# RWKV chunk operands of one layout for heads of both parities, and r and v projected inside the chunk loop, in a two-layer backbone on one core

## The chip, the cores and the metric

One Trainium2 chip, one of its cores. The time is device time in microseconds of one execution of the whole program; the number for a kernel is the median of several executions.

## What is computed

The program is a backbone of two layers over 512 latent and 256 context tokens. Layer 0 mixes by attention, layer 1 by two recurrences; each layer ends in a mixture of 64 experts. The change is in layer 1, in the bidirectional RWKV-7 mixing, whose reference is

```python
r, k, v, z_w, z_a, z_g = ... shift_mix(h @ w_in) ...      # p + mu * (mean of both neighbours - p)
decay = exp(-exp(-softplus(-w_pre) - 0.5)); iclr = sigmoid(...); kk = k * kvec[0] / norm
def rwkv7_step(state, inp):                    # per direction and head, over 768 tokens
    r, w, k, v, kk, a = inp
    sa = einsum('...vk,...k->...v', state, -kk)
    state = state * w + sa (x) (kk * a) + v (x) k
    return state, einsum('...vk,...k->...v', state, r)
```

with 8 heads of 64 channels, two directions, and an output gate and group norm behind it. A second recurrence (mLSTM, 4 heads of 128) runs beside it on other columns of the same projection.

## The kernel before, in words

The kernel computes the recurrence in chunks of 64 tokens. The head index is h = 2j + s: j is one of four 128-column blocks, s the half of the partitions (the parity). Layer 1 goes through four stages.

**Inputs** (`rec_mixed`, from L1673). `project` (L1584) multiplies one 128-column block of the weights with the normalised tokens: each product runs as three fp32r products (L414 to L416, high and low parts), over a context segment of 256 tokens and a latent segment of 512, in k-steps; the result lies in a two-bank PSUM tile `pp`, of which there are two. The weights' high part is cast on ACT (L1593), the low part made on POOL (L1594). `shifted` (L1678) copies the result to a padded tile, adds the neighbours on POOL (L1695), and `mix` (L1699) scales on ACT (L1703) and combines on DVE (L1704). This is done for z (4 blocks), k (4; its norm goes through the reciprocal L1754, and kk to DRAM at L1756), r (4, latent tokens only; L1758 to L1761) and v (4; transposed at L1771, stored to DRAM at L1776). The mLSTM gates (`mlstm_gates`) are a generator of 12 steps, taken one at a time in the loops over k, r and v.

**Chunk loop** (`rec_chunks`, from L2004, called in L1617 to L1621). Six pairs of chunks b and two directions d. `prep` makes the operands: tanh (L2077), plus one on POOL (L2078), a cumulative sum (L2081), two exponentials, the copy of the chunk's last decay to PL (L2088), then ST (L2100 from kk on DVE, L2102 from r on POOL) and BK (L2112, L2113). ST and BK are written by one instruction for each partition half s, since the two parities have their 64-column parts in opposite order (FA, FR in L2011). `pairs` multiplies BK with ST for each chunk q, j and s (L2149; the matmul has L394, the line of the helper `crit`), copies Aab out on ACT (L2154), and masks the rest into ST and Arb on DVE (L2156, L2160), again for each half; it stores Aab, ST, Arb and BT to DRAM with one DMA per tile (`put`, L2048, its issue has L2054). `invert` inverts 16-wide blocks (L2194, L2196) and `merge` joins them (products T, Q, W, TT). The products of each go through PSUM banks `pb` (four of them).

`weave` (L294) draws the steps of several generators in proportion to their stated lengths; that is the order of the program. In the same weaves run the 80 steps of `mlstm_project` (L1781), the projections of the mLSTM's q, k, v and o, in portions written out by hand: `take(9)`, `take(6)`, then 7 and 6. The compiler's scheduler fixes each engine's order in advance from a simulated timeline, with the program's order as priority; at run time every engine keeps that order.

**Rest of the chunks** (L1628, L1629) beside the first mLSTM cells. **Scan** (`rwkv_scan`, from L2245): 12 steps in each direction, that load the chunks' operands, multiply (px), copy X out of PSUM in two halves (L2293), multiply, copy the new V (L2306), update the state (L2319, L2322) and copy or add the output y in two halves (L2334, L2336). `self.copy` takes ACT and DVE in turn (L387, L389). Five steps run beside the mLSTM cells, the others beside a part of the output projection.

After it come the output projection, the router and the second layer's experts, which the change does not touch.

Of the kernel before, what the change touches and what calls it, by code (L numbers as in the profile page):

```python
# [26 lines left out]
NCTX = 256  # L27
# [79 lines left out]
def constants_rec():  # L107
# [6 lines left out]
    low = (p < 64)[:, None]  # L114
    both = [np.where(low, np.concatenate([incl[d], strict[d]], 1), np.concatenate([strict[d], incl[d]], 1))
            for d in range(2)]
# [239 lines left out]
class Kern:  # L356
# [1178 lines left out]
    def rec_project(self, es, x, R):  # L1535
# [72 lines left out]
        with tc.tile_pool(name="rt", bufs=1, reuse_waits="tile") as tp:  # L1608
            self.rec_mixed(tp, project, mu2, nkv, low, r, k_, R)
# [63 lines left out]
    def rec_mixed(self, tp, project, mu2, nkv, low, r, k_, R):  # L1673
# [45 lines left out]
        for j in range(4):  # L1719
            cur = shifted(12 + j, (CT, LT))  # L1720
# [20 lines left out]
        for j in range(4):  # L1741
            next(gates)
# [15 lines left out]
        for j in range(4):  # L1758
            next(gates)
            cur = shifted(j, (LT,))  # L1760
            mix(cur, 0, j, LT, r[:, j])  # L1761
        for j in range(4):
            next(gates, None)
            cur = shifted(8 + j, (CT, LT))
            vT, vt = z(), z()
            for sl in (CT, LT):
                mix(cur, 2, j, sl, vT[:, sl])
            for t0 in (0, 3):
                p = self.bank((128, 3, 128))
                for t in range(3):  # L1770
                    nc.tensor.transpose(p[:, t], vT[:, (t0 + t) * 128:(t0 + t + 1) * 128], self.k_ident)  # L1771
                self.copy(vt[:, t0 * 128:t0 * 128 + 384], p.rearrange("p a b -> p (a b)"))
            next(gates, None)
            for q in range(2):
                for s in range(2):
                    nc.sync.dma_start(R["V"][q::2, s, :, j * 64:(j + 1) * 64].rearrange("c p v -> p c v"),  # L1776
                                      vt[64 * q:64 * q + 64].rearrange("p (c s v) -> p c s v", c=6, s=2)[:, :, s])
# [3 lines left out]
    def mlstm_project(self, tp, project, R):  # L1781
# [5 lines left out]
        def stage(name, n=NTOK, bufs=2):  # L1787
            return tp.tile([128, n], F32, name=name, tag=name, bufs=bufs)
# [13 lines left out]

        for h in range(4):
# [200 lines left out]
    def rec_chunks(self, gp, low, up, kv2, wa2, r, k_, R):  # L2004
# [6 lines left out]
        FA, FR = (half[0], half[1]), (half[1], half[0])  # L2011
# [32 lines left out]
        def par(v, s):  # L2044

            return v.rearrange("p c (j e) t -> p c j e t", e=2)[:, :, :, s]

# [10 lines left out]
        def prep(b, d):  # L2058
# [19 lines left out]
            nc.gpsimd.tensor_scalar(sw, sw, 1.0, None, op0=add)  # L2078
# [12 lines left out]
            ST = tmp("ST", 3, (128, 2, 8, 128))  # L2091
            ST = ST.rearrange("p q h t -> p (q h t)")[:, 0:16 * w].rearrange("p (q h t) -> p q h t", q=2, h=8)
            BK = tmp("BK", 2, (128, 4, 2, 128))
            SA = FA if lat else (half[0], half[0])
            jc = lambda v, s: two(v[half[s]])
            cj = lambda v, s: jc(v, s).rearrange("p j c t -> p c j t")
            dj = lambda v, s: v[half[s]].rearrange("p j c t -> p c j t")
# [13 lines left out]
            for s in range(2):  # L2111
                nc.vector.tensor_tensor(BK[half[s], :, :, FR[s]], jc(ke, s), jc(E2, s), op=mult)  # L2112
                nc.vector.scalar_tensor_tensor(BK[half[s], :, :, FA[s]], jc(aa, s), -0.5, jc(E2, s), op0=mult, op1=mult)  # L2113
            P[b, d] = dict(ST=ST, BK=BK, SA=SA, kk=kk, ke=ke)
# [21 lines left out]
        def pairs(b, d):  # L2136
            lat = b >= 2
            ST, BK, SA = (P[b, d][n] for n in ("ST", "BK", "SA"))
            Aab = tmp("Aab", 4, (128, 2, 4, 64))
            Arb = tmp("Arb", 2, (128, 2, 4, 64)) if lat else None  # L2140
            BT = tmp("BT", 2, (128, 2, 4, 128))

            cs = [slice(0, 128) if lat else FA[s] for s in range(2)]
            ss = [slice(0, 128) if lat else SA[s] for s in range(2)]
            for q in range(2):
                p = self.pair((128, 2, 4, 128))
                for j in range(4):
                    for s in range(2):
# [3 lines left out]
                for s in range(2):  # L2152
                    bh, kh = half[s], half[1 - s]
                    nc.scalar.copy(Aab[bh, q], p[bh, s, :, FA[s]])  # L2154
                    mask = self.k_both[kh, d, cs[s]]
                    nc.vector.tensor_tensor(par(ST[kh], s)[:, q, :, ss[s]], p[kh, s, :, cs[s]],  # L2156
                                            mask[:, None].to_broadcast([64, 4, mask.shape[-1]]), op=mult)
                    if lat:
                        mask = self.k_incl[bh, d]
                        nc.vector.tensor_tensor(Arb[bh, q], p[bh, s, :, FR[s]],  # L2160
                                                mask[:, None].to_broadcast([64, 4, 64]), op=mult)
# [10 lines left out]
            for q in range(2):  # L2172
                p = self.bank((128, 4, 128))
                for j in range(4):
                    self.crit_t(p[:, j], BK[:, j, q], self.k_ident)
                nc.scalar.copy(BT[:, q], p)
                yield
            put(b, d, 1024, BT)
# [66 lines left out]
    def rwkv_scan(self, room, R):  # L2245
# [4 lines left out]
        half = FA = (slice(0, 64), slice(64, 128))  # L2250
# [20 lines left out]
        def step(n, d, Y):  # L2271
# [4 lines left out]
            ST = L[:, 1024 - 8 * w:1024].rearrange("p (h t) -> p h t", h=8)  # L2276
            BT = L[:, 1024:1536].rearrange("p (j t) -> p j t", j=4)
# [5 lines left out]
            if n < 11:  # L2283
                load(n + 1, d)
            px = self.bank((128, 2, 4, 64))
# [178 lines left out]
```

## Time and profile before

| | us |
|---|---|
| median of 3 executions | 2880.4 |
| lowest, highest | 2874.06, 2880.7 |
| the profiled execution | 2889.01 |
| its span, first to last instruction | 2887.2 |

| engine | busy us | share of the span |
|---|---|---|
| PE (matmul) | 2426.5 | 84% |
| PEld (weight load) | 1477.0 | 51% |
| DVE | 1214.1 | 42% |
| ACT | 705.5 | 24% |
| POOL | 661.6 | 23% |

The mean granted clock of TensorE over the span is 0.900 of full speed. Shares over the span mix stages of different limits; layer 1's recurrence lies between about 1400 and 2140 us. An engine's instructions overlap in the timeline, so the busy time of a group is a sum of durations and not a share of the span, while an engine's own busy time in a window counts each moment once.

### The profile page before, as it was taken

What the parts mean: (1) busy time and instruction counts of PE and PEld (TensorE: products, weight loads), DVE (VectorE), ACT (ScalarE), POOL (GpSimd) and SP (SyncE); (2) the same over time, 40 slices, a digit from 0 to 9 for tenths busy, and PEclk for the clock granted to TensorE, in tenths of its full rate; (3) what the DMA queues carried; (4) which work ended last, traced back from release to release, by engine and by line L of the source; (5) the groups of instructions that cost most, each with busy time, mean ns of one, the idle gap of its engine ahead of it and who ended that gap; (6) DMA issues with size and microseconds to landing.
All of it is one profiled execution on the core that took longest, in us unless ns stands there. A gap on an engine that the chain in (4) does not pass through costs nothing. (4 is left out here: it accounts for less than half of the span.)

```text
span 2887.2 us, 45906 instructions
## 1 busy us (share of the span) xinstructions
PE 2426.5 (84%) x18031; PEld 1477.0 (51%) x18031; DVE 1214.1 (42%) x2625; ACT 705.5 (24%) x1556; POOL 661.6 (23%) x618
## 2 busy tenths in 40 slices
PE   7789887979999999994899777766866989988993
PEld 6658664864433443331678666666755323323331
DVE  5742545472122222214753677755576211212214
ACT  3442434231111111112544433412212100000001
POOL 0111010002112122111344454534530111111211
PEclk9899998879999999997899788868966999999996
DMA  8645444659999999995224445588644998999995
GB/s 313 221 126 128 100 132 110 249 224 337 379 342 329 356 338 342 382 347 179 84 75 108 134 128 156 157 223 276 235 163 167 386 396 336 361 395 353 340 406 186
DMA packets 253865, 721.91 MB, mean 250 GB/s; under 512 B 110968, under 2 KB 137336, under 8 KB 194512
## 3 DMA queue, kind: packets, MB, share of 16 engines
q1 hardware_dynamic: 216656, 631.86, 59.7%
q0 software_dynamic: 26336, 67.70, 9.4%
q10 hardware_dynamic: 10656, 19.40, 2.0%
q8 instruction: 143, 2.34, 0.4%
q14 instruction: 74, 0.61, 0.1%
HBM read 636.06 MB, written 107.33 MB: 257 GB/s over the span
## 5 line engine op out<-in xcount | busy, mean ns | idle before, releaser
L1235 PE MATMUL pb<-ew,xT 128*32 128x512 f32 (+2 forms) x3504 | 656.2, 607 | 21.5 <-DMA ew<-in_moe_w_dram 14.7
L1235 PEld LDWEIGHTS pb<-ew,xT 128*32 128x32 f32 (+2 forms) x3504 | 212.0, 127 | 394.5 <-issue 354.9
L1235 PE MATMUL pp<-ew,hT 128*32 128x512 f32 (+2 forms) x1752 | 330.6, 607 | 13.1 <-DMA ew<-in_moe_w_dram 6.0
L1456 DVE SCALAR_TENSOR_TENSOR hs<-s,gate,pb 128x256 f32<-128x256 f32 x86 | 41.3, 480 | 608.0 <-ACT s L1451 596.7
L1225 POOL DMA_INDIRECT xg<-rows,idx x86 | 89.0, 1035 | 857.4 <-PE pp L1279 300.3
L1451 ACT ACTIVATE s<-pb 128x256 f32<-128x256 f32 x96 | 36.3, 383 | 815.0 <-PE pb L1235 785.4
L1270 POOL DMA_INDIRECT acc<-ye,idx x86 | 136.9, 1591 | 327.8 <-issue 109.9
L1235 PEld LDWEIGHTS pp<-ew,hT 128*32 128x32 f32 (+2 forms) x1752 | 101.6, 127 | 194.1 <-issue 174.3
L414 PE MATMUL pp<-h_hi,w_hi 128*128 128x512 f32 (+1 forms) x432 | 161.3, 375 | 4.8 <-DVE mT L389 4.3
L415 PE MATMUL pp<-h_lo,w_hi 128*128 128x512 f32 (+1 forms) x432 | 158.7, 368 | 1.1 <-DVE h_lo L410 1.1
L416 PE MATMUL pp<-h_hi,w_lo 128*128 128x512 f32 (+1 forms) x432 | 158.9, 369 | 0.6 <-POOL w_lo L1594 0.6
L1594 POOL TENSOR_TENSOR w_lo<-w,w_hi 128x512 fp32r<-128x512 f32 x66 | 93.3, 1415 | 170.1 <-ACT w_hi L1593 100.0
L1279 PEld LDWEIGHTS pp<-consts,xg 128*128 128x128 f32 x688 | 79.9, 147 | 77.0 <-issue 55.7
L1279 PE MATMUL pp<-consts,xg 128*128 128x128 f32 x688 | 99.1, 290 | 20.8 <-DMA xg<-rows,idx 7.6
L440 PE MATMUL pb<-ada_w,cz 128*32 128x256 f32 x640 | 56.1, 471 | 52.6 <-DMA ada_w<-in_ada_w_dram 52.6
L414 PEld LDWEIGHTS pp<-h_hi,w_hi 128*128 128x128 f32 x432 | 86.0, 200 | 20.5 <-DVE mT L389 4.4
L1282 DVE COPY xT<-pp 128x512 f32<-128x512 f32 x86 | 59.3, 690 | 88.2 <-ACT xT L1281 88.2
L416 PEld LDWEIGHTS pp<-h_hi,w_lo 128*128 128x128 f32 x432 | 85.5, 198 | 16.3 <-issue 3.4
L415 PEld LDWEIGHTS pp<-h_lo,w_hi 128*128 128x128 f32 x432 | 86.2, 199 | 14.9 <-issue 2.2
L414 PE MATMUL pb<-w_hi,m_hi 128*128 128x256 f32 x256 | 76.8, 303 | 11.6 <-ACT w_hi L409 11.6
L1281 ACT COPY xT<-pp 128x512 f32<-128x512 f32 x86 | 50.3, 585 | 147.7 <-PE pp L1279 146.5
L598 PE MATMUL pb<-consts,P 128*128 128x128 f32 x384 | 70.6, 301 | 9.9 <-ACT P L854 5.3
(515 smaller groups left out, 4610.9 us busy)
## 6 DMA issues: line engine op xcount, KB each, us to landing
ew<-in_moe_w_dram SPq DMA_DIRECT2D x384, 1024.0 KB
ada_w<-in_ada_w_dram SPq DMA_DIRECT2D x48, 1024.0 KB
w<-in_rec_w_dram ACTq DMA_DIRECT2D x66, 256.0 KB
steps<-dL SPq DMA_DIRECT2D x16, 1024.0 KB
acc<-zero SPq DMA_DIRECT2D x12, 1024.0 KB
ew<-acc SPq DMA_DIRECT2D x10, 1024.0 KB
w<-in_att_w_dram SPq DMA_DIRECT2D x18, 512.0 KB
cells<-dM SPq DMA_DIRECT2D x8, 1056.0 KB
```

The lines of the kernel that those rows point to most:

```text
L414: mm(out, l_hi, r_hi, start=start, stop=False)
L415: mm(out, l_hi, r_lo, start=False, stop=False)
L416: mm(out, l_lo, r_hi, start=False, stop=stop)
L440: nc.tensor.matmul(p[32 * g:32 * g + 32], self.cz[:, 4 * a + g, 30 - 2 * i:62 - 2 * i], w[:, 4 * a + g, :], start=i + a == 0, stop=i + 1 = ...
L598: nc.tensor.transpose(t[:, c - c0, :], p[:, c * 128:(c + 1) * 128], self.k_ident)
L1225: nc.gpsimd.indirect_dma_start(out=xg, out_offset=None, in_=self.rows[layer], in_offset=bass.IndirectOffsetOnAxis(ap=idx, axis=0), bounds_ ...
L1235: nc.tensor.matmul(out[s], x[:, s], ws[m], start=start, stop=stop, tile_position=(0, s.start))
L1270: nc.gpsimd.indirect_dma_start(out=self.acc[layer], out_offset=bass.IndirectOffsetOnAxis(ap=idx, axis=0), in_=y, in_offset=None, bounds_ch ...
L1279: columns_of.last = nc.tensor.transpose(p[:, k], xg[:, k * 128:(k + 1) * 128], self.k_ident[:n, :n])
L1281: nc.scalar.copy(out[:, 0:4], p[:, 0:4])
L1282: columns_of.done = nc.vector.tensor_copy(out[:, 4:8], p[:, 4:8])
L1594: nc.gpsimd.tensor_tensor(lo, w, hi.bitcast(F32), op=OP.subtract)
```

## The change

The two parts of ST are now in the order of their source (tensor index o: 0 from kk and r, 1 the masked product), and the same for both parities; so each of the instructions that wrote one half of the partitions is now one for both. Products in `pairs` are split in two: 64 columns of BK at a time, with the output in the half `s ^ o`. The stores of ST and BT to DRAM are split in three each. The decay's last column is made by an exponential on ACT and not copied by DVE; plus one moves from POOL to ACT. In the scan X and y leave PSUM with one instruction each. r and v leave `rec_mixed` and become the first 48 steps of the generator woven into the chunk loop, now of 128 steps; the portions become 13, 9, then 11 and 9, and 60 in the last weave. Gate steps are taken two at a time in the loops over z and k.

```diff
-            blocks = self.mlstm_project(tp, project, R)
+            blocks = self.rec_others(tp, project, mu2, r, R)
...
-                weave(W("prep", at(m), 0), W("pairs", at(m - 1), 1), W("merge", at(m - 2)), take(7 if m else 9))
+                weave(W("prep", at(m), 0), W("pairs", at(m - 1), 1), W("merge", at(m - 2)), take(11 if m else 13))
...
-                      W("bonus", at(m - 1) if m > 2 else None), take(6))
-            weave(W("pairs", at(5), 1), W("merge", at(4)), take(40))
+                      W("bonus", at(m - 1) if m > 2 else None), take(9))
+            weave(W("pairs", at(5), 1), W("merge", at(4)), take(60))
...
         for j in range(4):
+            next(gates)
+            next(gates)
             cur = shifted(12 + j, (CT, LT))
...
-        for j in range(4):
-            next(gates)
-            cur = shifted(j, (LT,))
-            mix(cur, 0, j, LT, r[:, j])
...
+        for j in range(4):
+            yield from shifted(j, 0, j, (LT,), lambda sl, t: r[:, j])
+        for j in range(4):
+            got = []
+            yield from shifted(8 + j, 2, j, (CT, LT), lambda sl, t: got.append(t) or t)
+            vt = tp.tile([128, 6, VW], F32, name="mt", tag="mt", bufs=1)
...
-            nc.gpsimd.tensor_scalar(sw, sw, 1.0, None, op0=add)
+            nc.scalar.activation(sw, sw, AF.Identity, bias=1.0, scale=1.0)
...
+            nc.scalar.activation(R["PL"][:, d, 2 * b:2 * b + 2].rearrange("p q j -> p j q"),
+                                 two(sw)[..., 63 * (1 - d)], AF.Exp, scale=LAM)
             nc.scalar.activation(E2, sw, AF.Exp, scale=-LAM)
-            nc.vector.tensor_copy(R["PL"][:, d, 2 * b:2 * b + 2].rearrange("p q j -> p j q"), E3[..., 63 * (1 - d)])
...
-            for s in range(2):
-                dst = par(ST[half[s]], s)
-                nc.vector.tensor_tensor(dst[:, :, :, SA[s]], dj(E1, s), cj(kk, s), op=mult)
-                if lat:
-                    nc.gpsimd.tensor_tensor(dst[:, :, :, FR[s]], dj(E3, s), cj(r[:, :, ls], s), op=mult)
+            nc.vector.tensor_tensor(ST[:, :, 0, :, half[0]], dj(E1), cj(kk), op=mult)
+            if lat:
+                nc.gpsimd.tensor_tensor(ST[:, :, 0, :, half[1]], dj(E3), cj(r[:, :, ls]), op=mult)
...
-                    for s in range(2):
-                        self.crit(p[:, s, j, cs[s]], BK[half[s], j, q], ST[half[s], q, 2 * j + s, ss[s]],
-                                         start=True, stop=True, tile_position=(64 * s, 0))
+                    for o in range(2):
+                        for s in range(2):
+                            self.crit(p[half[s ^ o], o, j, 0:w], BK[half[s], j, q, half[o]], ST[half[s], q, 0, j],
+                                      start=True, stop=True, tile_position=(64 * s, 64 * (s ^ o)))
...
+                nc.scalar.copy(Aab[:, q], p[:, 0, :, half[0]])
+                mask = self.k_both[:, d, 0:w]
+                nc.vector.tensor_tensor(ST[:, q, 1], p[:, 1, :, 0:w], mask[:, None].to_broadcast([128, 4, w]), op=mult)
...
-            put(b, d, 0 if lat else 512, ST)
+            nc.sync.dma_start(Ld[half[0], :, at:at + 8 * w], ST[half[0]].rearrange("p q o j t -> p q (o j t)"))
+            for o in range(2):
+                a = at + 4 * w * (1 - o)
+                nc.sync.dma_start(Ld[half[1], :, a:a + 4 * w], ST[half[1], :, o].rearrange("p q j t -> p q (j t)"))
...
             X, S = Xs[d], Ss[d]
-            for s in range(2):
-                self.copy(X[half[s]], px[half[s], s])
+            self.copy(X, px[:, 0])
```

BK's writers and the adding and copying of y are joined in the same way as ST and X, and BT's store is split like ST's. In `rec_others` the padded tile and its neighbour sum both come from the tag `mT` of two buffers, which the mLSTM's stages use too, and v's transposed tile from `mt` of one buffer.

## Rows read from the trace of the kernel before

**Rows 1.** Windows view: inputs, chunk loop, scan; busy us (instructions) per engine, clock, DMA.
```profile
1400.00:1564.60 164.60, 159.74 (x817) 125.99 (x817) 79.69 (x87) 78.10 (x132) 74.71 (x107) 0.98 0.25 75
1564.60:1885.00 320.40, 245.68 (x2275) 206.81 (x2275) 228.06 (x404) 128.67 (x320) 155.87 (x107) 0.82 0.52 144
...
1968.00:2140.00 172.00, 131.16 (x1980) 111.45 (x1978) 107.28 (x259) 44.02 (x102) 84.39 (x92) 0.84 0.67 224
```

**Rows 2.** Timeline of PE inside two projections: start us, us, what; first and last of runs.
```profile
1498.69 0.39 PE L414 MATMUL pp<-h_hi,w_hi 128*128 128x512 f32 x1
...
1503.73 0.39 PE L415 MATMUL pp<-h_lo,w_hi 128*128 128x512 f32 x1
...
1525.14 0.28 PE L414 MATMUL pp<-h_hi,w_hi 128*128 128x256 f32 x1
...
1526.38 0.28 PE L416 MATMUL pp<-h_hi,w_lo 128*128 128x256 f32 x1
```

**Rows 3.** Groups by form, inputs stage (busy us, mean ns | idle before, releaser).
```profile
L1771 PE MATMUL pb<-consts,z 128*128 128x128 f32 x24 | 3.9, 272 | 0.0
...
L1754 DVE RECIPROCAL z<-z 128x768 f32<-128x768 f32 x4 | 19.8, 4950 | 3.9 <-ACT z L1753 3.9
```

**Rows 4.** Waits in the chunk loop: who for whom, us in total, times, longest.
```profile
ACT Aab L2154 <- DVE Arb L2160: 42.8, 12, 7.5
...
PE pp L394 <- DVE ST L2156: 13.1, 3, 6.7
...
PE pb L1799 <- DVE mT L389: 11.7, 1, 11.7
```

**Rows 5.** Groups of DVE in the chunk loop, by form; the last over 1565 to 1900.
```profile
L2113 DVE SCALAR_TENSOR_TENSOR BK<-aa,sw 64x512 f32<-64x512 f32 x24 | 25.6, 1066 | 0.1
L2100 DVE TENSOR_TENSOR ST<-decay,kk 64x512 f32<-64x512 f32 x24 | 24.5, 1019 | 0.2
L2112 DVE TENSOR_TENSOR BK<-ke,sw 64x512 f32<-64x512 f32 x24 | 23.8, 993 | 2.8 <-POOL ke L2109 2.4
...
L2156 DVE TENSOR_TENSOR ST<-pp,consts_rec 64x512 f32<-64x512 f32 x28 | 19.2, 686 | 12.6 <-ACT Aab L2154 12.2
...
L2160 DVE TENSOR_TENSOR Arb<-pp,consts_rec 64x256 f32<-64x256 f32 x28 | 11.8, 422 | 0.6
L2088 DVE COPY PL<-decay 128x8 f32<-128x8 f32 x12 | 10.8, 898 | 0.9 <-ACT decay L2086 0.8
...
L2229 DVE TENSOR_TENSOR W<-pb,T 128x512 f32<-128x512 f32 x9 | 6.2, 688 | 2.5 <-PE pb L394 2.3
```

**Rows 6.** Groups of POOL in the chunk loop, by form.
```profile
L2102 POOL TENSOR_TENSOR ST<-decay,rk 64x512 f32<-64x512 f32 x16 | 24.5, 1528 | 0.6
...
L2078 POOL TENSOR_SCALAR sw<-sw 128x512 f32<-128x512 f32 x12 | 18.0, 1498 | 35.8 <-ACT sw L2077 32.4 <-PE pp L394 3.2 <-DVE W L2229 0.2
```

**Rows 7.** Timeline of PE: products of the chunks, 64-row operands.
```profile
1674.40 1.16 PE L394 MATMUL pp<-ST,BK 64*128 64x128 f32 x16
...
1678.86 1.15 PE L394 MATMUL pb<-T,Aab 64*64 64x64 f32 x32
...
1718.25 2.08 PE L394 MATMUL pp<-ST,BK 64*128 64x128 f32 x16 [1.78 <-ACT mT L387]
```

**Rows 8.** Scan: a wait in total, and the timeline of one pair of copies.
```profile
ACT steps L387 <- DVE steps L389: 51.6, 35, 6.2
...
2064.44 0.42 DVE L389 COPY steps<-pb 64x256 f32<-64x256 f32 x1
...
2064.94 0.37 ACT L387 COPY steps<-pb 64x256 f32<-64x256 f32 x1 [0.90 <-DVE steps L389]
```

**Rows 9.** SP's queue: an issue, issue time of a kind (min/median/max ns), a wait.
```profile
1514.89 0.36 SPq L1756 DMA_DIRECT2D dK<-z  x1
...
L2054 SPq DMA_DIRECT2D dL<-BT x12: 359/463/1235, 1597.3 to 1920.9; - x12
...
SPq L2164 <- ACT Aab L2154: 42.8, 9, 17.9
```

More of the change, by code (lines that the diff above doesn't have):

```diff
@@ L113, in constants_rec @@
     far = (s // 16) != (t // 16)[None, :]
-    low = (p < 64)[:, None]
-    both = [np.where(low, np.concatenate([incl[d], strict[d]], 1), np.concatenate([strict[d], incl[d]], 1))
-            for d in range(2)]
+    both = [np.concatenate([strict[d], incl[d]], 1) for d in range(2)]
     c["far"] = np.concatenate([strict[0] & far, strict[1] & far], 1)
@@ L1671, in out_ahead, with rec_mixed @@
             yield
-    def rec_mixed(self, tp, project, mu2, nkv, low, r, k_, R):
+    def rec_mixed(self, tp, project, mu2, nkv, low, k_, R):
         nc, i = self.nc, self.i
@@ L1741, in rec_mixed @@
         for j in range(4):
-            next(gates)
+            next(gates, None)
+            next(gates, None)
             cur = shifted(4 + j, (CT, LT))
@@ L1757, in rec_mixed, with rec_others @@
                               kn.rearrange("p (b t) -> p b t", b=6))
-        for j in range(4):
-            next(gates)
-            cur = shifted(j, (LT,))
-            mix(cur, 0, j, LT, r[:, j])
[L1762 to L1774, printed above, removed]
-                for s in range(2):
-                    nc.sync.dma_start(R["V"][q::2, s, :, j * 64:(j + 1) * 64].rearrange("c p v -> p c v"),
-                                      vt[64 * q:64 * q + 64].rearrange("p (c s v) -> p c s v", c=6, s=2)[:, :, s])
         for _ in gates:
             pass
-    def mlstm_project(self, tp, project, R):
+    def rec_others(self, tp, project, mu2, r, R):
         nc = self.nc
@@ L1785, in mlstm_project, with stage, shifted @@
         M = R["M"]
-        def stage(name, n=NTOK, bufs=2):
-            return tp.tile([128, n], F32, name=name, tag=name, bufs=bufs)
+        def stage(name, n=NTOK):
+            return tp.tile([128, NTOK + 4], F32, name=name, tag=name, bufs=2)[:, :n]
+        def shifted(b, n, j, segs, dst):
+            pad, sh = stage("mT", NTOK + 4), stage("mT")
+            nc.gpsimd.memset(pad[:, 0:1], 0.0)
+            nc.gpsimd.memset(pad[:, NCTX + 1:NCTX + 3], 0.0)
+            nc.gpsimd.memset(pad[:, NTOK + 3:NTOK + 4], 0.0)
+            at = lambda sl, n=1: slice(sl.start + n + 2 * (sl.start > 0), sl.stop + n + 2 * (sl.start > 0))
+            yield from project(b, lambda sl, p: nc.scalar.copy(pad[:, at(sl)], p), segs)
+            for sl in segs:
+                t = sh[:, sl]
+                nc.gpsimd.tensor_tensor(t, pad[:, at(sl, 0)], pad[:, at(sl, 2)], op=OP.add)
+                nc.scalar.activation(t, t, AF.Copy, scale=mu2[:, 0, n, j:j + 1])
+                nc.vector.scalar_tensor_tensor(dst(sl, t), pad[:, at(sl)], mu2[:, 1, n, j:j + 1], t,
+                                               op0=OP.mult, op1=OP.add)
+            yield
         c6 = lambda v: v.rearrange("p (c t) -> p c t", c=v.shape[1] // 128)
@@ L2147, in pairs @@
                 for j in range(4):
-                    for s in range(2):
-                        self.crit(p[:, s, j, cs[s]], BK[half[s], j, q], ST[half[s], q, 2 * j + s, ss[s]],
-                                         start=True, stop=True, tile_position=(64 * s, 0))
+                    for o in range(2):
+                        for s in range(2):
+                            self.crit(p[half[s ^ o], o, j, 0:w], BK[half[s], j, q, half[o]], ST[half[s], q, 0, j],
+                                      start=True, stop=True, tile_position=(64 * s, 64 * (s ^ o)))
                 yield
[L2152 to L2161, printed above, removed]
+                nc.scalar.copy(Aab[:, q], p[:, 0, :, half[0]])
+                mask = self.k_both[:, d, 0:w]
+                nc.vector.tensor_tensor(ST[:, q, 1], p[:, 1, :, 0:w], mask[:, None].to_broadcast([128, 4, w]), op=mult)
+                if lat:
+                    nc.vector.tensor_tensor(Arb[:, q], p[:, 0, :, half[1]],
+                                            self.k_incl[:, d, None].to_broadcast([128, 4, 64]), op=mult)
                 yield
@@ L2175, in pairs @@
                     self.crit_t(p[:, j], BK[:, j, q], self.k_ident)
-                nc.scalar.copy(BT[:, q], p)
+                nc.scalar.copy(BT[:, q].rearrange("p s j v -> p j s v"), p.rearrange("p j (s v) -> p j s v", s=2))
                 yield
-            put(b, d, 1024, BT)
+            nc.sync.dma_start(Ld[:, :, 1024:1280], BT[:, :, 0].rearrange("p q j v -> p q (j v)"))
+            for s in range(2):
+                nc.sync.dma_start(Ld[half[1 - s], :, 1280:1536], BT[half[s], :, 1].rearrange("p q j v -> p q (j v)"))
             P[b, d] = dict(A=Aab, kk=P[b, d]["kk"], ke=P[b, d]["ke"])
@@ L2287, in step @@
                 j, s = h // 2, h % 2
-                self.crit(px[half[s], s, j], ST[:, h, FA[s] if lat else half[0]], V[:, s, j], start=h < 2,
+                self.crit(px[half[s], 0, j], ST[:, s, j, half[0]], V[:, s, j], start=h < 2,
                                  stop=not lat, tile_position=(0, 64 * s), skip_group_check=True)
@@ L2330, in step @@
                 y = Y[:, c - 4]
-                for s in range(2):
-                    o = half[1 - s]
-                    if n <= 7:
-                        self.copy(y[o], px[o, s])
-                    else:
-                        nc.vector.tensor_tensor(y[o], y[o], px[o, s], op=add)
+                if n <= 7:
+                    self.copy(y, px[:, 1])
+                else:
+                    nc.vector.tensor_tensor(y, y, px[:, 1], op=add)
                 yield
```

54 lines of the change are left out of this document (30 added, 24 removed).

## The prediction, made before the changed kernel was run

> **What bounds the kernel now.** I read the windows first, since shares over the whole span mix stages [rows 1]. In the inputs stage, 164.6 us, PE is busy for 159.7 of them at a granted clock of 0.98: nothing but PE work sets its length. In the chunk loop, 320.4 us, no engine is full: PE 245.7, DVE 228.1, POOL 155.9, ACT 128.7, at a clock of 0.82. There 74.7 us of PE's time are idle, and part of the rest runs at the lower of the two clock levels: the same 16 instructions take 1.16 us at one place and 2.08 at another [rows 7]. The scan, 172.0 us, is full on no engine either.
>
> The waits of the loop tell why [rows 4]. ACT's copy of Aab stood 42.8 us behind DVE's Arb, which reads another half of the same PSUM tile, so the readers of a product take turns; PE in turn waited 13.1 us for the mask product on DVE to free the tile, and 11.7 us in one piece for a projection's copy in DVE's queue. The groups of DVE show the load [rows 5]: ST and BK are written by 24 half-height instructions each, 73.9 us in three groups. A full-height product of 512 columns costs 688 ns and a half-height one 686 ns: height is free, so two halves joined cost one.
>
> **The change, part by part.** *r and v leave the inputs stage.* One latent matmul of 512 columns follows the next after (1503.73 - 1498.69) / 22 = 0.229 us, a context one of 256 columns after (1526.38 - 1525.14) / 11 = 0.113 us [rows 2]. A block has 24 of each. r: 4 x 24 x 0.229 = 22.0 us. v: 4 x 24 x (0.229 + 0.113) = 32.8 us. v's transposes: 24 x 272 ns, less the overlap that a duration contains, about 3 us [rows 3]. Together 58 us, and since that stage is all PE, it gets shorter by these 58. Against it stands its new end: the k blocks each carry a reciprocal of 4.95 us on DVE [rows 3], and the last store of kk, issued at 1514.89 [rows 9], stood some 50 us ahead of the loop's start; now the loop's first operands need it at once. r's projections cover that for PE. I charge 3 us, bounds 0 and 10 (two reciprocals). The gates' steps, now two at a time, are DVE work inside a stage of some 109 us that has at most 79.7 us of it: 0; if DVE fell behind there, z's products would wait for it, up to the same 10.
>
> *The same 58 us of PE work enter the loop.* The rest of r and v comes with it: weight loads on ACT's queue, casts, low parts and neighbour sums on POOL, scaling on ACT, combining on DVE, 16 stores on SP. r and v are 8 of the 17 blocks of the inputs stage, so at most half of what that stage has: ACT 39 us, POOL 37, DVE (79.7 - 19.8) / 2 = 30 [rows 1, 3].
>
> *DVE gets lighter.* Joined halves: 73.9 / 2 = 37.0 for ST and BK, 9.6 for the mask, 5.9 for Arb; PL's copy leaves, 10.8 [rows 5]. That is 63 us off 228.1, plus at most 30 from r and v: under 196 us. *POOL* loses 18.0 (plus one) and 12.2 (half of ST) [rows 6] and gains up to 37: under 163. *ACT* gains up to 39, plus one (bounded by POOL's 18.0) and twelve small exponentials, and loses half of the Aab copies: under 190. All three stay below two thirds of 320.
>
> *The products in pairs double in number.* A latent pass (16 of them: 4 chunk pairs, 2 directions, 2 chunks) has 8 products of 128 columns now, 1.16 us; afterwards 16 with half the weights' width. T's row has 16 products of 64 x 64 in 1.15 us [rows 7]: 16 products can be no dearer than twice 1.16 and hardly cheaper than once. Extra: 0 to 16 x 1.16 = 18.6; the 8 context passes take T's form exactly, extra 0 to 9, and I take 0 by that row. In sum 9 us, bounds 0 and 28.
>
> The Trainium skill, TensorEngine Tiling (Array Packing), section Tiling Modes, says that four 64 x 64 tiles load and multiply independently of each other. By that the extra would be 0 and PE's work 9 us less; no row of before has four such tiles in turn.
>
> *SP* issues 48 more DMAs (two each for ST and BT, 12 times) and v's 16: 64 x 0.46 = 30 us. It is in order; in the loop it waited 42.8 us for Aab alone [rows 9], so the issues fit there, but a store in front of the inversion's load delays it by about 1 us a pair. I take 0; without that cover it would be 30.
>
> *What the loop then takes.* PE: 245.7 + 58 + 9 = 313 us at the present clock mix. At a mean of 0.82 between 0.5 and 1, some 36% of the time is at the lower level, and so 88 us of the 245.7, which would take half at the upper: 269 to 313, about 290 if the extra filling lifts the clock halfway. Nothing else is near. The lower bound is 269 / 0.97, the filling of the inputs stage: 277, 43 shorter than now. The upper is everything on top: 320 + 67 = 387. I take 320, no change, which is 290 at 91% filling: better than now, since the readers of a product no longer queue (two banks, each with its own reader first) and the waits for DVE lose their cause, but not the inputs stage's 97%, since pairs and projections share two PSUM tiles. Likely 295 to 345.
>
> *Scan.* X left PSUM by DVE at 2064.44 and then by ACT until 2065.31; such turns cost ACT 51.6 us of waiting [rows 8]. One copy of 0.42 saves 0.45 us in each of 24 steps: 0 to 10.8. As two directions run beside each other, half: 5. y's joined copies lie off the chain; I cost them at 0.
>
> Sum: -58 + 3 + 0 - 5 = **-60 us**. The profiled execution took 2889.0, so 2829 in its terms; it lies 8.6 above the median of 2880.4, which gives 2820. A difference under 0.3% (8.6 us) can't be told from none.
>
> **The rivals.** *The loop hangs on its chain, not on PE.* Then lighter DVE and POOL shorten it although PE has more to do, down to its bound of 277: -58 + 3 - 43 - 5 = -103, that is 2777. For it: the idle 74.7 us, and every wait of [rows 4] is on something that shrinks. Against: it needs PE full almost throughout, in a program order whose waits vary.
>
> *The work is only moved.* If PE's idle time can't be filled, since it lies where filling is not allowed (a projection needs one of two PSUM tiles that pairs hold), the loop takes 387: -58 + 3 + 67 - 5 = +7, that is 2887, within 0.3% of before; halfway it would be 2854. For it: PE waited although projections were there to be run. Against: the product's readers now free the tiles sooner.
>
> *Slower: projections that wait to be evacuated.* r and v leave PSUM through padded tiles that share two buffers with the mLSTM's stages, sum and all; the next block's copy waits until the block before is combined on DVE, and the tile of PSUM stays taken meanwhile. Before, one such wait for a copy cost PE 11.7 us in one piece [rows 4]. If the work is moved without filling, and one in three of the 24 blocks waits so long, 8 x 11.7 = 94: 2887 + 94 = 2981. From the forecast, it decides from 60 / 11.7, five such waits, on. Against: only one in 16 blocks before, and DVE is lighter.
>
> **How the numbers follow.** Forecast (loop 295 to 345, so 2795 to 2845): 0.62. Chain rival, 2795 and below: 0.17. Only moved, 2845 to 2889: 0.15. Slower: 0.06. The likeliest gives **2820**. The range 2783 to 2858 takes in the forecast, nearly all of the chain rival and the better third of the third case, and with it the bounds of the pairs (9 down, 19 up) and the new end (3, 7). Faster by over 0.3%: 0.62 + 0.17 and 0.09 of the third, 0.88; within: 0.06; slower: 0.06.
>
> **What would show it.** The inputs stage ends near 1508 with PE over 90% busy until then; the loop, from there to the last chunk pair's preparation, takes 295 to 345 us with PE above 270 busy and a clock above 0.82; DVE in it is under 200; the half-height forms of ST, BK, mask and Arb are gone and the full-height ones cost the same 0.7 to 1.1 us; ACT's wait for Arb falls below half of 42.8; scan steps are shorter by some tenths. Wrong would be: full-height forms that cost twice the half-height ones, a latent pass in pairs above 2.3 us, or long waits of PE for a projection's copy.

## The result, and the profile after

The changed kernel takes 2808.1 us (median of 4 runs, 2803.6 to 2820.5), the kernel before 2880.6 beside it (4 runs): a ratio of 0.976, 95% interval 0.974 to 0.979. The forecast was 2820 in a range of 2783 to 2858. The profiled execution of the changed kernel has a span of 2805.0 us, that of before 2887.2.

First the page's busy times, then the windows view by stage (start:end, length, busy us and instructions of PE, PEld, DVE, ACT, POOL, then granted clock, DMA share, GB/s): the end of the inputs, the chunk loop, the rest up to the scan, the scan.

```profile
span 2805.0 us, 46569 instructions
...
PE 2392.1 (85%) x18415; PEld 1441.5 (51%) x18415; DVE 1138.2 (41%) x2513; ACT 696.3 (25%) x1540; POOL 636.0 (23%) x598
```

```profile
1393.00:1501.30 108.30, 103.56 (x503) 77.25 (x503) 61.57 (x68) 54.66 (x90) 44.27 (x57) 0.98 0.19 61
1501.30:1833.30 332.00, 289.72 (x3049) 240.51 (x3048) 188.45 (x343) 150.38 (x367) 161.65 (x138) 0.93 0.64 163
1833.30:1896.90 63.60, 47.04 (x654) 43.58 (x655) 35.36 (x91) 9.13 (x20) 27.04 (x25) 0.88 0.82 254
1896.90:2053.70 156.80, 120.39 (x1962) 103.17 (x1962) 93.83 (x224) 37.52 (x83) 84.94 (x93) 0.89 0.71 241
```

The loop of [rows 1] ends at 1885.0; up to the event at which the loop is cut here, the last Arb, it and the rest behind it are in the kernel before:

```profile
1564.60:1890.50 325.90, 250.26 (x2320) 210.64 (x2321) 232.06 (x412) 130.72 (x325) 157.78 (x108) 0.82 0.53 146
1890.50:1968.30 77.80, 55.80 (x683) 51.63 (x684) 38.44 (x91) 9.01 (x19) 28.57 (x29) 0.76 0.73 219
```

So PE is busy for 39.5 us longer in the loop, at a clock of 0.93 in place of 0.82, and VectorE for 43.6 us less. The inputs end earlier with PE about as full as before (103.6 of 108.3 us).

To compare kernels I cut each at the same events: the first transposition of the inputs, the first product of the chunks' preparation (the loop begins), the last Arb (it ends), the scan's first load, the last sum of y. In us:

| | before | after | difference | moved only | operands only |
|---|---|---|---|---|---|
| earlier layers, unchanged | 1358.7 | 1351.7 | -7.0 | 1358.0 | 1357.6 |
| inputs | 205.9 | 149.6 | -56.3 | 149.3 | 203.4 |
| chunk loop | 325.9 | 332.0 | +6.1 | 376.8 | 303.4 |
| rest up to the scan | 77.8 | 63.6 | -14.2 | 70.9 | 68.2 |
| scan | 167.9 | 156.8 | -11.1 | 162.8 | 149.4 |
| what follows, unchanged | 751.0 | 751.3 | +0.3 | 752.9 | 751.0 |

The last two columns are the first two experiments. The first line is the same code in all fourteen executions and lies between 1347.3 and 1363.4; single totals carry that much, so causes are read from the stages.

The groups of DVE in the loop, by form (busy us, mean ns of one | idle before, its releaser), answer to [rows 5]:

```profile
L2120 DVE SCALAR_TENSOR_TENSOR BK<-aa,sw 128x512 f32<-128x512 f32 x12 | 18.3, 1524 | 0.2
L2119 DVE TENSOR_TENSOR BK<-ke,sw 128x512 f32<-128x512 f32 x12 | 17.9, 1492 | 1.6 <-POOL ke L2117 1.2 <-ACT sw L2098 0.3
L2108 DVE TENSOR_TENSOR ST<-decay,kk 128x512 f32<-128x512 f32 x12 | 11.7, 976 | 2.1 <-ACT decay L2095 1.5 <-DMA kk<-dK 0.5
L2162 DVE TENSOR_TENSOR ST<-pp,consts_rec 128x512 f32<-128x512 f32 x16 | 10.9, 679 | 3.3 <-ACT Aab L2160 3.3
...
L2164 DVE TENSOR_TENSOR Arb<-pp,consts_rec 128x256 f32<-128x256 f32 x15 | 6.2, 412 | 0.0
```

Half as many instructions each. The mask and Arb, which read PSUM, take what a half took (679 and 412 ns). ST and BK together fall from 73.9 us to 47.9, not to half: ST halves (24.5 to 11.7), but BK only goes from 49.4 to 36.2, for its mean rose from 1.0 to 1.5 us.

The waits of the loop (who for whom, us in total, times, longest) answer to [rows 4]:

```profile
POOL BK L2180 <- PE pp L392: 67.6, 7, 15.3
...
DVE As L2201 <- DMA Tb<-dA: 23.9, 5, 6.9
...
ACT Aab L2160 <- PE pp L392: 12.9, 5, 5.0
...
DVE ST L2162 <- ACT Aab L2160: 11.0, 7, 6.0
...
PE pp L392 <- DVE ST L2162: 7.9, 2, 5.0
...
PE pp L412 <- ACT mT L1778: 5.5, 2, 3.1
...
DVE aa L2116 <- DMA kk<-dK: 3.0, 1, 3.0
```

ACT's 42.8 us behind Arb are gone: Aab now waits for the product itself. POOL's 67.6 are idle time of an engine that is not full. VectorE waits 23.9 us for the inversion's load, 7.8 before. The products of the pairs in PE's timeline, a context and a latent pass, answer to [rows 7]:

```profile
1542.45 0.69 PE L392 MATMUL pp<-ST,BK 64*64 64x64 f32 x32
...
1643.01 1.10 PE L392 MATMUL pp<-ST,BK 64*64 64x128 f32 x32 [1.10 <-DVE BK L2120]
1643.91 1.13 PE L392 MATMUL pb<-T,Aab 64*64 64x64 f32 x32
```

and a context pass before:

```profile
1601.04 1.11 PE L394 MATMUL pp<-ST,BK 64*128 64x64 f32 x16
```

Twice the products take 1.10 us in a latent pass, where 1.16 stood; a context pass takes 0.69, and took 1.11 before.

### The profile page after: what moved, and what is told of

Read it like the earlier page. It is cut to its first block, busy times and chain, and to the rows that moved or that the text cites. A ratio compares the mean times of both kernels' runs of the same rounds, so it can differ in the third digit from the quotient of the medians.

```text
span 2805.0 us, 46569 instructions
## 1 busy us (share of the span) xinstructions
PE 2392.1 (85%) x18415; PEld 1441.5 (51%) x18415; DVE 1138.2 (41%) x2513; ACT 696.3 (25%) x1540; POOL 636.0 (23%) x598
## 5 line engine op out<-in xcount | busy, mean ns | idle before, releaser
L1277 PE MATMUL pp<-consts,xg 128*128 128x128 f32 x688 | 98.8, 289 | 18.5 <-DMA xg<-rows,idx 6.6
L413 PEld LDWEIGHTS pp<-h_lo,w_hi 128*128 128x128 f32 x432 | 86.3, 200 | 14.6 <-issue 2.8
```

Of the source, the lines that this page charges most:

```text
L413: mm(out, l_hi, r_lo, start=False, stop=False)
L1277: columns_of.last = nc.tensor.transpose(p[:, k], xg[:, k * 128:(k + 1) * 128], self.k_ident[:n, :n])
```

## The experiments

Each is one edit of the changed kernel unless it says otherwise. "The loop" is the stage cut as above, 332.0 us in the changed kernel.

**The move alone.** The operands of the kernel before (its constants, chunk preparation and scan) with the projections of r and v in the loop (of the diff against the changed kernel, two places):

```diff
+        FA, FR = (half[0], half[1]), (half[1], half[0])
...
-            nc.vector.tensor_tensor(BK[..., half[1]], two(ke), two(E2), op=mult)
...
+            for s in range(2):
+                nc.vector.tensor_tensor(BK[half[s], :, :, FR[s]], jc(ke, s), jc(E2, s), op=mult)
...
```

> r and v go into the chunk loop, operands and scan as before. The inputs stage loses 56 us in both theories. Theory 1 (PE's idle time in the loop takes the work, and the joined operands are a gain of their own): the loop grows by 10 us at most, its PE share rises from 77% to over 88%, total near 2835. Rival (the idle time could only be filled because DVE got lighter and the readers of a product no longer queue): DVE has 232 us and some 20 more in the loop, which grows by 30 to 55 us, total 2855 to 2880.

2872.2 us, ratio 0.998 (0.996 to 1.000): almost nothing. Its loop, and in it the wait that joined operands were to remove:

```profile
1507.30:1884.10 376.80, 305.29 (x2675) 254.97 (x2676) 267.63 (x432) 154.38 (x367) 193.58 (x159) 0.86 0.53 145
```

```profile
ACT Aab L2170 <- DVE Arb L2176: 29.8, 13, 6.0
```

The inputs give 56.6 us and the loop takes 50.9 of them back, as the rival expected. With the old operands the prediction's rival "only moved" was nearly true.

**The operands alone.** The kernel before with the new constants, preparation and scan; r and v stay among the inputs (the diff is against the changed kernel):

```diff
-                weave(W("prep", at(m), 0), W("pairs", at(m - 1), 1), W("merge", at(m - 2)), take(11 if m else 13))
+                weave(W("prep", at(m), 0), W("pairs", at(m - 1), 1), W("merge", at(m - 2)), take(7 if m else 9))
...
```

> Operands and scan as after, r and v still in the inputs stage. Theory 1: the loop was held by DVE and by the turns of the readers, so it gets shorter by itself, by 20 to 40 us, the rest of the chunks by 10 and the scan by 10: total 2825 to 2845. Rival (the loop hangs on its round trips through DRAM and on the projections' pace, not on DVE): the loop keeps its 326 us, total 2855 to 2865.

2837.2 us, ratio 0.986 (0.981 to 0.990): theory 1.

```profile
1561.00:1864.40 303.40, 241.09 (x2774) 201.47 (x2773) 170.62 (x331) 127.43 (x326) 120.76 (x90) 0.86 0.67 165
```

The loop gets 22.5 us shorter, rest and scan 9.6 and 18.5. The two parts need each other in the loop: the same move costs 376.8 - 325.9 = 50.9 us with the old operands and 332.0 - 303.4 = 28.6 with the new ones, about half of the 58 us of PE work that it brings. The traces show the difference as idle time of PE in the loop, which the move leaves as it is with the old operands (75.6 to 71.5 us) and cuts with the new ones (62.3 to 42.3). Of PE's waits in the loop, those for VectorE sum to 56.0 us before, 53.1 with the move alone, 46.9 with the operands alone and 24.7 with both.

**The scan's copies in halves.**

```diff
-            self.copy(X, px[:, 0])
+            for s in range(2):
+                self.copy(X[half[s]], px[half[s], 0])
...
-                if n <= 7:
-                    self.copy(y, px[:, 1])
+                for s in range(2):
+                    o = half[1 - s]
+                    if n <= 7:
+                        self.copy(y[o], px[o, 1])
```

> As after, but X and y leave PSUM in two halves again. If the joined copies are what made the scan 11 us shorter, the scan is 165 to 170 us again and the total 2815 to 2820; nothing else moves. If the scan was shorter for another reason (other order, earlier loads), it stays at 157 us and 2808.

2818.2 us, 0.979 (0.975 to 0.983); the scan takes 166.4 us in place of 156.8. The wait of ACT for VectorE in the scan, first the changed kernel, then this one (before: 51.6, [rows 8]):

```profile
ACT steps L385 <- DVE steps L387: 21.6, 15, 5.0
```

```profile
ACT steps L385 <- DVE steps L387: 52.2, 36, 4.8
```

24 steps of 0.45 us are 10.8: the joined copies, X's and y's together, are worth nearly the whole of that, not half. The scan takes 149.4 to 157.8 us in the eleven kernels with joined copies and 162.8 to 167.9 in the three with halves.

**Plus one back on GpSimd, PL back on VectorE.**

```diff
-            nc.scalar.activation(sw, sw, AF.Identity, bias=1.0, scale=1.0)
+            nc.gpsimd.tensor_scalar(sw, sw, 1.0, None, op0=add)
...
-            nc.scalar.activation(R["PL"][:, d, 2 * b:2 * b + 2].rearrange("p q j -> p j q"),
-                                 two(sw)[..., 63 * (1 - d)], AF.Exp, scale=LAM)
...
+            nc.vector.tensor_copy(R["PL"][:, d, 2 * b:2 * b + 2].rearrange("p q j -> p j q"), E3[..., 63 * (1 - d)])
```

> As after, but plus one is on POOL again and PL is copied by DVE. DVE gets some 11 us and POOL 18 us more in the loop, ACT 10 less, and each preparation waits about 1 us longer for POOL. If DVE and POOL are off the path now that PE fills the loop: 2805 to 2815. If the preparation's chain sets the loop: 12 times 1 to 2 us, 2820 to 2832.

2819.8 us, 0.980 (0.976 to 0.985).

```profile
1499.60:1843.00 343.40, 293.06 (x3049) 242.50 (x3048) 201.34 (x357) 143.57 (x343) 176.82 (x151) 0.91 0.63 160
```

The loop takes 11.4 us more, and the total lies between the two expectations. Two small edits to which the prediction gave no gain of their own may be worth as much as the scan's.

**ST and BK in halves**, with the new layout and the products as they are:

```diff
-            nc.vector.tensor_tensor(ST[:, :, 0, :, half[0]], dj(E1), cj(kk), op=mult)
+            for s in range(2):
+                o = half[s]
+                nc.vector.tensor_tensor(ST[o, :, 0, :, half[0]], dj(E1[o]), cj(kk[o]), op=mult)
...
-            nc.vector.tensor_tensor(BK[..., half[1]], two(ke), two(E2), op=mult)
...
+            for s in range(2):
+                o = half[s]
+                nc.vector.tensor_tensor(BK[o, :, :, half[1]], two(ke[o]), two(E2[o]), op=mult)
...
```

GpSimd's part of ST (from r) and BK's second product are split in the same way.

> As after, but ST and BK are written by one instruction for each half again (layout, products and the masks stay joined). Of the loop's instructions 36 on DVE and 8 on POOL come back, some 26 and 12 us. If the load of DVE and POOL and the length of a preparation are what the joined layout bought in the loop (theory 1), it grows by 12 to 30 us, total 2820 to 2838. If it bought room by the readers of a product no longer taking turns (rival), it stays within 5 us: 2808 to 2813.

2858.4 us, 0.993 (0.991 to 0.995): 50 us of the 72 are gone, more than either theory allowed. The loop, 38.8 us longer, with VectorE busy for 49.1 us more:

```profile
1513.00:1883.80 370.80, 304.50 (x3049) 252.20 (x3048) 237.59 (x380) 151.02 (x367) 175.56 (x146) 0.88 0.58 146
```

**The readers of the products in halves too** (Aab, mask, Arb):

```diff
-                nc.scalar.copy(Aab[:, q], p[:, 0, :, half[0]])
...
+                for s in range(2):
+                    o = half[s]
+                    nc.scalar.copy(Aab[o, q], p[o, 0, :, half[0]])
...
```

> As prep_halves, and Aab, the mask product and Arb are read from PSUM in halves too, in the old order, so the readers take turns on one bank again. DVE gets 13 us more and ACT 8. Theory 1: 8 to 15 us above prep_halves. Rival: this is the step that costs, 20 us or more above prep_halves; both together give back the 22 us by which layout_only's loop is shorter than that of before, and as much as 45 where r and v are in it.

2882.6 us, 1.002 (1.001 to 1.004): the whole gain is gone, with r and v still moved. Its loop takes 397.6 us, 26.8 more than with ST and BK alone, as the rival of this experiment expected, and the old wait is back, between pieces of one operand:

```profile
ACT Aab L2166 <- DVE Arb L2171: 40.7, 13, 12.2
```

**BK alone in halves, and GpSimd's part of ST alone in halves**, to see which of the two made the 39 us (of the experiment on ST and BK, the first takes only the lines of both BK products, the second only the line that writes r's part of ST).

> The changed kernel, but both products of BK on VectorE in two instructions of 64 partitions each: 24 more instructions of 0.7 to 1.5 us, 17 to 36 us more for VectorE, GpSimd's work as it is. With r's half of ST and the rest of ST this made 39 us together. Theory 1, VectorE's queue is what the loop hangs on beside PE: the loop gets longer by 17 to 36 us, 349 to 368. Rival, GpSimd's halves made most of the 39: less than 12, so under 344.

> The changed kernel, but r's half of ST, written by GpSimd, in two instructions of 64 partitions: 8 more instructions of about 1.49 us on GpSimd, 12 us more, VectorE's work as it is. Theory 1, what cost 39 us with all of ST and BK in halves is VectorE's own queue: the loop stays within 5 us of 332. Rival, it is GpSimd, beside which VectorE's instructions take up to 1.76 us in place of 0.68: the loop gets longer by 12 to 25 us, and VectorE's mean times rise with no instruction of its own added.

```profile
1506.30:1871.90 365.60, 307.31 (x3049) 253.80 (x3048) 217.78 (x368) 151.28 (x367) 163.19 (x138) 0.86 0.58 148
```

```profile
1499.60:1842.60 343.00, 291.18 (x3049) 241.23 (x3048) 188.48 (x344) 149.98 (x367) 169.09 (x146) 0.94 0.62 158
```

BK: 2850.7 us, 0.989 (0.987 to 0.990). VectorE has 29.3 us more to do and the loop takes 33.6 more: theory 1, and most of the 39. PE runs the same 3049 instructions, but for 307.3 us at a clock of 0.86 where it was 289.7 at 0.93: 17.6 of the 33.6 are PE being busy for longer, the other 16 its idle time. GpSimd: 2820.6 us, 0.979 (0.974 to 0.984), the loop 11.0 longer, between the two expectations; VectorE's busy time did not move (188.48), so the rival's mechanism is not in it, and neither the 11.0 us of one loop nor the total can be told from the changed kernel's.

**VectorE loaded with sums that nobody reads.**

```diff
             nc.vector.scalar_tensor_tensor(BK[..., half[0]], two(aa), -0.5, two(E2), op0=mult, op1=mult)
+            dead = tmp("dead", 1, (128, 4))
+            for n in range(4):
+                nc.vector.tensor_reduce(out=dead[:, n:n + 1], in_=flat(ke), op=add, axis=mybir.AxisListType.X)
```

> The changed kernel with 48 instructions more on VectorE whose results nobody reads: four sums over 512 columns of ke after each chunk pair's BK, some 0.6 us each, 29 us, as much as the halves of BK added (29 us, for which the loop took 34 us more). They stand in VectorE's queue at the place where BK's halves stood, but no instruction waits for their results; what follows in the queue comes later by them. Theory 1, VectorE is in order and the loop hangs on what comes round in its queue: the loop takes 20 to 35 us more, 352 to 367. Rival, the loop hangs on the length of the steps of one preparation, ST and BK up to the products, and VectorE has time to spare beside it (188 of 332 us busy): less than 10 us more, under 342.

2836.1 us, 0.987 (0.983 to 0.991). The loop, and three groups of VectorE in it:

```profile
1496.90:1850.90 354.00, 296.64 (x3049) 246.37 (x3048) 211.00 (x392) 151.04 (x367) 155.03 (x138) 0.89 0.60 153
```

```profile
L2123 DVE TENSOR_REDUCE dead<-ke 128x1 f32<-128x512 f32 x48 | 29.6, 671 | 0.1
...
L2119 DVE TENSOR_TENSOR BK<-ke,sw 128x512 f32<-128x512 f32 x12 | 14.9, 1238 | 0.0
L2120 DVE SCALAR_TENSOR_TENSOR BK<-aa,sw 128x512 f32<-128x512 f32 x12 | 14.5, 1206 | 1.5 <-ACT sw L2098 1.5
```

The sums are 29.6 us, but BK got cheaper beside them (29.4 in place of 36.2), so VectorE's total grew by 22.5, and the loop by 22.0. Theory 1: work that nobody waits for is paid in full, though VectorE is busy for only 211 of 354 us. Of the 22.0 us, PE is busy for 6.9 and idle for 15.1. The wait of PE that grew most is for W, a sum of VectorE's in `merge`, first in the changed kernel, then here:

```profile
PE pb L392 <- DVE W L2242: 3.9, 4, 2.9
```

```profile
PE pb L392 <- DVE W L2245: 12.9, 3, 6.9
```

All of PE's waits for VectorE rise from 24.7 to 35.0 us, those for ACT's copies to the padded tile from 5.5 to 14.6; but the waits for the mask and Arb, which stand behind the sums too, fall from 9.6 to 5.9. That the sums delay what follows them in VectorE's queue fits this; which instruction carries the delay on to PE is not shown.

**Copies of projections to ACT alone**, the opposite test, and an attempt at a better version: `self.copy(...)` becomes `nc.scalar.copy(...)` in the function that projects r, v and the mLSTM's blocks.

```diff
-                self.copy(vt[:, t0:t0 + n, 0:128], p)
+                nc.scalar.copy(vt[:, t0:t0 + n, 0:128], p)
...
```

> The changed kernel, but every copy of a projection or of its transposes out of PSUM (k, v and the output gate of the mLSTM, v of the chunks), which ACT and VectorE take in turns, goes to ACT alone. Nothing else is changed, and the sum of the work stays. In the chunk loop of the changed kernel VectorE is busy for 188.5 of 332.0 us and ACT for 150.4. Theory 1, PE's gaps are filled as far as VectorE, behind which the copies stand, comes round: some 12 us leave VectorE, and the loop gets shorter by 5 to 12 us (320 to 327, total about 2798). Rival, only the chain of the preparation counts, and ACT stands in it as well (gates, decays, Aab): the loop stays within 4 us of 332, or gets longer by up to 8 as ACT's queue now holds what PE waits for.

2815.1 us, 0.977 (0.975 to 0.978).

```profile
1499.00:1839.10 340.10, 292.75 (x3049) 244.81 (x3048) 172.77 (x322) 159.21 (x389) 156.45 (x138) 0.91 0.63 161
```

VectorE has 15.7 us less, ACT 8.8 more, and the loop is 8.1 longer: the rival. So the loop does not follow VectorE's sum either way: copies taken out of its queue freed nothing here. Whether the 8.1 us are the price of the copies in ACT's queue is not shown; one loop may differ by so much (see the limit below).

**Every product of the pairs four times**, with the same result:

```diff
-                for j in range(4):
+                for j in [0, 1, 2, 3] * 4:
```

> As after, but every product of BK with ST is run four times over, into the same place. A latent pass takes 1.10 us and a context pass 0.69, so PE gets 3 x (16 x 1.10 + 8 x 0.69) = 69 us more. If PE bounds the loop now (290 us busy of 332), the loop grows by 50 to 69 us: total 2858 to 2877. If it is held by the chain and the queues of the other engines, half of that or less: under 2843.

2918.8 us, 1.015 (1.012 to 1.019). Both expectations missed: the loop takes 434.8 us, 102.8 more. PE's busy time grew by 65.6 of these and its idle time by the other 37.2; the largest of its waits is new:

```profile
L392 PE MATMUL pp<-ST,BK 64*64 64x128 f32 x2048 | 77.8, 302 | 26.7 <-DVE Arb L2164 26.7
```

The product stands in the chain from preparation to mask to the next product. Work put there cost more than its length, where the projections beside it cost half of theirs.

**One projection step less in each weave.**

```diff
-                weave(W("prep", at(m), 0), W("pairs", at(m - 1), 1), W("merge", at(m - 2)), take(11 if m else 13))
+                weave(W("prep", at(m), 0), W("pairs", at(m - 1), 1), W("merge", at(m - 2)), take(10 if m else 12))
...
-                      W("bonus", at(m - 1) if m > 2 else None), take(9))
+                      W("bonus", at(m - 1) if m > 2 else None), take(8))
```

> The changed kernel with one projection step less taken beside each of the twelve weaves (12, 10 and 8 in place of 13, 11 and 9), so that 12 steps of the mLSTM's projections run after the loop instead of in it. Theory 1, PE's work in the loop is what the loop pays for at about half its length (28 us for 58): 12 steps of some 1 to 1.5 us leave it, the loop gets shorter by 5 to 10 us and what follows longer by as much or less, total 2800 to 2812. Rival, the steps fill gaps of PE that stay open otherwise: the loop stays within 4 us of 332, the rest gets longer by 10 to 18, total 2818 to 2828.

2841.5 us, 0.988 (0.985 to 0.990): both missed. VectorE's running sum opens each of the twelve preparations; first and last start, in the changed kernel and then here:

```profile
L2090 DVE TENSOR_TENSOR_SCAN sw<-reset,sw x12: 1207/1596/2531, 1509.6 to 1806.2; 128x512 f32<-128x512 f32 x12
```

```profile
L2090 DVE TENSOR_TENSOR_SCAN sw<-reset,sw x12: 1203/1224/2435, 1516.3 to 1822.6; 128x512 f32<-128x512 f32 x12
```

From first to last it is 306.3 us in place of 296.6: with less work of PE beside them the preparations come no faster, but slower. The loop as a whole:

```profile
1507.40:1873.90 366.50, 300.07 (x3145) 251.96 (x3144) 180.44 (x345) 151.50 (x368) 154.43 (x138) 0.87 0.58 147
```

It is 34.5 us longer, and the step that both expectations took for granted failed: the twelve steps did not leave the loop. Each of the three projection lines has as many products in it as in the changed kernel, 176 of 512 columns and 96 of 256. The last weave takes up to 60 steps and had only 6 left of the 128; now it has 18, and it stands ahead of the last Arb. The last pair, woven with them, has its last Arb 51.3 us after the last running sum (1873.9 - 1822.6) in place of 27.1 (1833.3 - 1806.2). What leaves the twelve weaves is not saved; it comes in the last one, and costs more there. What less work in the loop would give is left open.

Of the kernels run, the changed one is the fastest. Buffers of their own for the projections' padded tiles, in place of the two shared ones, do not fit: the pool would take 111.6 KB per partition where 99.8 are left. What the shared ones cost was not measured.

## Why the prediction held, point by point

- **Inputs, -58 + 3: held.** Measured -56.3. PE sets that stage, busy for 96% of its last 108 us, and its work could be counted.
- **Loop, no change: held, within its 25 us, at +6.1.** PE's work, forecast at 290, is 289.7, the clock rose from 0.82 to 0.93, VectorE is at 188 (under 196 forecast). That the work agrees to 0.3 us is luck: up to the last Arb the kernel before has 250.3 us and not 245.7, and the pairs brought -4 and not 9, so that the sum at the old clock is 304 and not 313; 14 us came off with the higher clock, where 23 were forecast. The filling is 289.7 / 332.0 = 87%, not 91. What the working did not show is how the zero comes about: the move costs 29 us and the operands give 22 without it and 45 with it (376.8 - 332.0).
- **Pairs, +9 (0 to 28): mis-sized, below its lower bound.** 16 latent passes at 1.10 in place of 1.16 and 8 context passes at 0.69 in place of 1.11 are -4 us. I had not counted that a context pass of four small tiles can beat one of two. T's row, whose form I took it to have, uses only two of the four tiles (in `merge` every product has the position (0, 0) or (64, 64)), and still takes 1.13 us. By the Trainium skill, TensorEngine Tiling (Array Packing), section Tiling Modes, the four tiles run independently, which gave an extra of 0; the trace agrees, and goes a little further.
- **VectorE, ST and BK halved, -37: mis-sized, -26.** ST halved, and so did the mask and Arb; all of the miss is BK's. "Height is free" came from rows with a source in PSUM; BK reads two tensors in SBUF, and what joining did not halve is its time beside GpSimd (see the last section). The sign "the full-height ones cost the same 0.7 to 1.1 us" failed there, with 1.5.
- **Plus one and PL: no gain of their own given.** Undoing them costs the loop 11.4 us, about as much as one loop may differ by itself.
- **Scan, -5: mis-sized, -11.1.** Halving the 10.8 for the other direction beside it was wrong: with halves copied again the scan lost 9.6, and ACT's wait went from 21.6 back to 52.2. The y copies were not separated from X's.
- **The new end of the inputs, 3: held.** The loop's first operands wait 3.0 us for kk, whose last store is issued at 1509.2, after the loop's first product at 1501.3.
- **SP, 0: left open.** VectorE's wait for the inversion's load, which goes through SP's queue, rose from 7.8 to 23.9 us in five waits. PE is not named behind it; what the 64 issues cost was not separated.
- **The rest, no term: -14.2.** PE is busy there for 47.0 us in place of 55.8, with 654 instructions in place of 683 and a clock of 0.88 in place of 0.76, and idle for 5.4 us less. Executions with the changed kernel's code in that stage take 63.6 to 76.9 us, so how much of the 14.2 the change gives is not shown.
- **Rivals.** "Only moved" would have been right for the move alone. "Slower" did not come: PE's waits for the copies of r and v to their padded tiles are two, 3.1 us at the longest, and it needed five of 11.7. "The loop hangs on its chain" was not the end, but half true: work added to VectorE's queue cost 22 us for 22.5 and 34 for 29, and to the product itself 103 for 66 on PE.

Term by term against the profiled executions: inputs 1.3 more than forecast, the loop 6.1 less, the scan 6.1 more, the rest 14.2 more. That makes -75.5 of -60; with 7.0 less in unchanged code and 0.3 more it is the -82.2 of the spans. The medians differ by 72.4. In this pair of executions what the forecast lacked is in the main the term for the rest; that the loop's 6.1 and the scan's cancel is luck.

One limit holds for all the sizes of the loop: each loop is that of one profiled execution, one kernel's own totals differ by up to 17 us (2803.6 to 2820.5), and every variant with the moved work came out longer than the changed kernel, also the one that took work from VectorE. An edit changes the order in which five queues meet, and some 10 us of a difference may be that alone; only what is well above it (the 51, 45, 34, 22 and 103) is shown.

## What to carry to other kernels

Idle time of PE is worth filling only when the engines that free its tiles can follow: here the same move gave 4.7 us with operands in halves (2876.9, the kernel before beside it, to 2872.2) and 29 with whole ones (2837.2 to 2808.1). Cost an instruction by a row with the same sources, not only the same shape. Before pricing an edit by an engine's busy share, ask what stands behind it in that queue: VectorE is busy for 57% of the loop, and still 22.5 and 29.3 us added to its queue cost 22.0 and 33.6, while 15.7 us of copies moved from it to ACT gave nothing.

## What the runs showed of the hardware

**Two SBUF sources beside GpSimd.** The timeline of the changed kernel: at the loop's start, with GpSimd idle but for three memsets of 0.1 us; in its middle; and near its end:

```profile
1516.46 0.68 DVE L2119 TENSOR_TENSOR BK<-ke,sw 128x512 f32<-128x512 f32 x1
...
1640.18 3.82 POOL L2128 TENSOR_TENSOR ke<-ke 128x512 f32<-128x512 f32 x1
...
1641.59 0.67 DVE L2119 TENSOR_TENSOR BK<-ke,sw 128x512 f32<-128x512 f32 x1
...
1809.84 1.65 POOL L2110 TENSOR_TENSOR ST<-decay,rk 128x512 f32<-128x512 f32 x1
...
1810.77 0.63 DVE L2162 TENSOR_TENSOR ST<-pp,consts_rec 128x512 f32<-128x512 f32 x1
...
1811.91 1.56 POOL L1592 TENSOR_TENSOR w_lo<-w,w_hi 128x512 fp32r<-128x512 f32 x1
1812.27 1.75 DVE L2119 TENSOR_TENSOR BK<-ke,sw 128x512 f32<-128x512 f32 x1
```

The same BK takes 0.68 us alone and 1.75 beside GpSimd; the mask, with one source in PSUM, takes 0.63 beside it. It is not always VectorE that is held up: at 1641.59 BK took 0.67 us beside GpSimd, and there GpSimd's ke took 3.82 us, where the one at 1813.44 took 1.74. With BK in halves a half-height one took as long as a joined one (675 ns at least, 1536 in the median, 24 times), and the 48 sums with their single source took 662 to 679 ns throughout. The Trainium skill, GPSIMD Engine Reference, section Specifications, says that GpSimd shares its SBUF interfaces with VectorE, with contention when a VectorE instruction has two SBUF inputs; the trace agrees, and puts 0.68 against 1.75 us on it.

**The clock takes part.** In the eight kernels whose loop has the same 3049 instructions of PE, its busy time goes with the clock: 289.7 us at a mean granted clock of 0.93, 296.6 at 0.89 and 307.3 at 0.86, the first with 42.3 us of idle time of PE in the loop, the others with 57.4 and 58.3. All eight lie at 288 to 293 us for 0.91 to 0.94 and at 297 to 307 for 0.86 to 0.89.
